# The operands of the first merge product requested during the last gate product

## The chip, the cores and the metric

The kernel runs on one core of a Trainium2 chip, as one program. The metric is the device time of one execution in microseconds (us), the median of several runs. Engines are named as in the profile: PE (TensorE's matmuls; its weight loads are listed as PEld), DVE (VectorE), ACT (ScalarE), POOL (GpSimd) and SP (SyncE, here the queue that issues most DMAs).

## What is computed

A decoder layer with three gated token mixers side by side, then cross-attention and an MLP. The change lies where the mixers are merged:

```python
u = rms_norm(h, norm_mix)
proj = u @ w_in
y_b = ssd_branch(...) @ w_ssd_out          # 2048 inner channels
y_c = swa_branch(...) @ w_attn_out         # sliding-window attention, 16 heads
gates = sigmoid(proj[..., OFF_GATE:] + gate_bias)     # 3 x 1024 columns
merged = gates[0] * y_a + gates[1] * y_b + gates[2] * y_c
h = h + merged @ w_mix_out
...
```

All is float32, 1024 tokens, model width 1024.

## The kernel before

Activations lie channel by channel: a [128, 1024] tile holds 128 channels of 1024 tokens, and a width of 1024 is eight such tiles. A float32 product is made of three products of rounded parts. An operand x is split into `oh`, a rounded copy written by ACT, and `ol`, the rest, written by DVE (`split`, lines 291 to 300: L295 and L296). A weight is split in the same way into `wh` and `wl` (`wslot`, L162 and L165 to L168). PE then adds wh x oh, wh x ol and wl x oh. `gemm_steps` does this for one output tile of 128 channels: for each of eight input tiles six matmuls of 512 tokens, and it yields after every third. So one product of 1024 x 128 has 16 steps, and two steps use up one input tile.

The normalised input u occupies eight pairs of split tiles: four in the pool `opa`, four in `opb`, and these pools have no other buffers. All products with u read them. Last among these are the 24 gate products. 21 of them (`gates_of`, 3 to 23) have no place of their own: they are filler. The generator `fillers` runs through them and then through `merge_head`, and the sliding-window attention calls `fill(n)` between its own small products, which advances the filler by 2n steps. A gate ends with a tanh on ACT (L324) into a tile `gate_th` of the pool `gp` (tag "glu", two buffers) and a store to `d_th` (L325).

`merge_head` is the beginning of the merge: the first two output tiles of y_b's first half. Its operands are the eight tiles `d_yb[0..7]`, which the SSD stage has stored to DRAM. For each one it requests a staging tile `yin` (even ones in `gp`, tag "glu", the gates' own; odd ones in `attn2`, two buffers), loads it (L336), and splits it into a pair of `opa` or `opb` (L295, L296). Those are the buffers that u holds until the last gate, number 23, has read them.

The attention goes through 16 blocks (8 groups of 128 queries, 2 halves of the heads). Iteration i transposes the probabilities of block i (`ps_pt`, L77, 8 at a time, twice; ACT copies them out, L1076), makes the scores of block i+2 (`ps_lg`, twice 8), and multiplies block i-1 by the values (`ps_o`). Between these stands one filler step each, four in an iteration. On the scores DVE adds the bias and takes the maximum (L1042) and makes the negated maximum `nm` and the sink's exponent `es` (L1050, L1051); ACT takes the exponentials (L1054, eight instructions); DVE sums and inverts (L1058, L1060); POOL multiplies the block `lg` by the inverse (L1061). All of these small products and the transposes share four PSUM buffers (`pss`). Gate 23 occupies iterations 10 to 13; `merge_head` begins in iteration 14, has eight of its 32 steps in iterations 14 and 15, and the rest at `fill(200)` after the attention.

What sets the order: PE's instructions are pinned in the order in which the program writes them (`Ordered`, `keep_in_program_order`). For the other engines a scheduler fixes the order beforehand. What is written in a `high_priority` block goes ahead of the rest as soon as its data and a buffer are there; a tile takes a buffer of its pool and tag when one is free. Each engine and each queue works through its list in order.

Of the kernel before, what the change touches and what calls it, by code (L numbers as in the profile page):

```python
# [9 lines left out]
F32 = mybir.dt.float32  # L10
# [7 lines left out]
P = 128  # L18
D = 1024
KT = D // P  # L20
T = 1024
# [7 lines left out]
START_GATES = 3  # L29
# [26 lines left out]
def trunk_kernel(tc, w_io):  # L56
    nc = tc.nc
    act, dve, pool = nc.scalar, nc.vector, nc.gpsimd
    ctx = ExitStack()
    with ctx:  # L60
# [57 lines left out]
        def C(name, i=0, n=1):  # L118
            o, w = _C[name]
            assert i + n <= w  # L120
            return cst[:, o + i:o + i + n]
# [9 lines left out]
        d_yb = dram.tile([16, P, T], F32, name="d_yb")  # L131
# [53 lines left out]
        def gemm_steps(slots, xh, xl, nk, pss_):  # L185


            for k in range(nk):
                wh, wl = slots(k)
                n = 0  # L190
                for stat, movs in ((wh, (xh, xl)), (wl, (xh,))):
                    for mv in movs:
                        for h in range(2):
                            sl = slice(h * 512, h * 512 + 512)
                            pe.matmul(
                                pss_[:, sl], stat, mv(k)[:, sl],
                                start=(k == 0 and stat is wh and mv is xh),
                                stop=(k == nk - 1 and stat is wl),
                            )
                            n += 1  # L200
                            if n % 3 == 0:
                                yield
# [8 lines left out]
        def ch_slots(src, cuts=(0, 1024)):  # L211
            wh, wl = wslot(src, cuts=cuts)
            return lambda k: (wh[:, k * P:(k + 1) * P], wl[:, k * P:(k + 1) * P])
# [71 lines left out]
        opa = ctx.enter_context(tc.tile_pool(name="opa", bufs=4))  # L285
        opb = ctx.enter_context(tc.tile_pool(name="opb", bufs=4))
        def pair(pool_):
            return (
                pool_.tile([P, T], F32R, tag="oh", name="oh"), pool_.tile([P, T], F32R, tag="ol", name="ol"),
            )  # L290

        def split(pool_, src, scale=None):
            a, b = pair(pool_)
            if scale is None:
                act.copy(a, src)  # L295
                dve.tensor_sub(b, src, a.bitcast(F32))  # L296
            else:
                act.activation(a, src, AF.Copy, scale=scale)
                dve.scalar_tensor_tensor(b, src, scale, a.bitcast(F32), ALU.mult, ALU.subtract)
            return a, b  # L300

        def hi(parts):
            return lambda k: parts[k][0]

        def lo(parts):
            return lambda k: parts[k][1]
# [4 lines left out]
        with ExitStack() as s1:  # L311
# [1 line left out]
            u = [pair(opa if k < 4 else opb) for k in range(KT)]  # L313
            UH, UL = hi(u), lo(u)

            def gates_of(n):
                for gt in n:
                    ps = pg.tile([P, T], F32, tag="g", name="ps_g")
                    steps = gemm_steps(ch_slots(w_io["w_ch"][40 + gt]), UH, UL, KT, ps)
                    for k in range(2 * KT):  # L320
                        next(steps)
                        if k == 2 * KT - 1:
                            th = gp.tile([P, T], F32, tag="glu", name="gate_th")
                            act.activation(th, ps, AF.Tanh, bias=C("gate_b", gt), scale=0.5)  # L324
                            nc.sync.dma_start(d_th[gt], th)  # L325
                        yield

            merging, staging = [], [gp]

            def merge_head():  # L330

                parts = []
                for k in range(KT):
                    with tc.high_priority():
                        y = staging[k % 2].tile([P, T], F32, tag="glu", name="yin")
                        nc.sync.dma_start(y, d_yb[k])  # L336
                        parts.append(split(opa if k < 4 else opb, y))
                two = [pg.tile([P, T], F32, tag="g", name="ps_g") for i in range(2)]
                sts = [gemm_steps(ch_slots(w_io["w_b0"][i]), hi(parts), lo(parts), KT, two[i]) for i in range(2)]
                merging.append((parts, two))  # L340
                for k in range(KT):
                    for st in sts:
                        for i in range(2):
                            next(st)
                            yield

            def fillers():
                yield from gates_of(range(START_GATES, 24))
                yield from merge_head()

            gates = fillers()

            filled = [0]
# [42 lines left out]
            with ExitStack() as sc:  # L396
# [117 lines left out]
                for s in range(4):  # L514

                    ps = pg.tile([P, T], F32, tag="g", name="ps_kv").rearrange("p (a b) -> p a b", b=512)
                    for kp in range(4):
# [5 lines left out]
                        for kk in range(2):  # L523
                            k = kp * 2 + kk
# [595 lines left out]
        with ExitStack() as sc:  # L1120
# [81 lines left out]
            parts = [split(opa if ct < 4 else opb, yconv[:, ct, :]) for ct in range(8)]  # L1202
# [5 lines left out]
        with tc.tile_pool(name="mix", bufs=2) as tp:  # L1208
            parts = [split(opa if i < 4 else opb, ht[i], 0.5) for i in range(KT)]
# [506 lines left out]
def build(nc, packed):  # L1716
    io = {k: nc.dram_tensor(k, v.shape, mybir.dt.from_np(v.dtype), kind="ExternalInput").ap() for k, v in packed.items()}
    io["outT"] = nc.dram_tensor("outT", (KT, P, T), F32, kind="ExternalOutput").ap()
    with tile.TileContext(nc) as tc:
        trunk_kernel(tc, io)  # L1720
# [12 lines left out]
```

## Time and profile before

| | us |
|---|---|
| runs before, median of 3 | 2727.51 |
| lowest, highest | 2725.08, 2733.04 |
| the profiled execution, time | 2729.99 |
| its span in the trace | 2728.0 |

The profiled execution took 2729.99 us, of which the trace shows a span of 2728.0 us. Times in the rows are microseconds from the start of the span. A row of the timeline reads: start, duration, engine, line, operation, tile written <- tiles read, shapes, count; in brackets how long the engine stood idle before it and what ended that. A row of the waits reads: who waited for whom, total, number, longest. A row of the stretches gives, for each engine in the order PE, PEld, DVE, ACT, POOL, its busy time and the number of its instructions, then the granted clock of TensorE as a share of the full one, the DMA engines' busy share and GB/s.

### The profile page before, as it was taken

Reading aid. Unit: us, or ns where it says so; the run is one execution under the profiler, and the core shown is the slowest. Engines: PE = TensorE matmul, PEld = TensorE weight load, DVE = VectorE, ACT = ScalarE, POOL = GpSimd, SP = SyncE. Lnnn points to the kernel's source line nnn. Section 1 sums busy time; section 2 is a strip of 40 time slices with the busy share of each in tenths; the row PEclk is TensorE's granted clock in tenths of the full one; section 3 lists DMA queues with packets and bytes.
Section 4 is the critical chain, followed back from the end, with each engine's and each line's share of the span. In section 5 each row is a group of like instructions: output and inputs, shape, how many; then the busy total and the mean of one; then the engine's idle time right before and its main releaser. Section 6 shows DMA issues by size and latency. Waiting matters only on the chain. (4 is left out here: it accounts for less than half of the span.)

```text
span 2728.0 us, 32485 instructions
## 1 busy us (share of the span) xinstructions
PE 2692.6 (99%) x12720; PEld 2180.4 (80%) x12720; DVE 1574.1 (58%) x1875; ACT 1097.1 (40%) x1827; POOL 794.1 (29%) x442
## 2 busy tenths in 40 slices
PE   9999999999999999999999999999998999999999
PEld 7888878888787878775588778899777888888887
DVE  7588878758667776524414774323368876532423
ACT  6533321225666666557611351235433332222221
POOL 2322221200504050424342422321115664422220
PEclk9999999999999999999999999999999999999999
DMA  7642232333555555572444332211123332454531
GB/s 241 210 128 97 97 112 88 123 124 85 147 162 143 145 151 153 177 218 82 149 170 160 101 109 100 101 55 40 47 77 116 139 131 106 175 194 142 202 137 70
DMA packets 119576, 354.83 MB, mean 130 GB/s; under 512 B 12016, under 2 KB 37120, under 8 KB 119040
## 3 DMA queue, kind: packets, MB, share of 16 engines
q1 hardware_dynamic: 112656, 328.12, 34.6%
q0 software_dynamic: 6768, 24.64, 5.2%
q8 instruction: 100, 1.64, 0.2%
q14 instruction: 52, 0.43, 0.1%
HBM read 277.06 MB, written 78.80 MB: 130 GB/s over the span
## 5 line engine op out<-in xcount | busy, mean ns | idle before, releaser
L73 PE MATMUL ps_g<-oh,wh 128*128 128x512 f32 x1776 | 575.8, 404 | 8.5 <-ACT oh L295 3.9
L73 PE MATMUL ps_g<-ol,wh 128*128 128x512 f32 x1776 | 562.0, 394 | 3.5 <-DVE ol L296 2.4
L73 PE MATMUL ps_g<-oh,wl 128*128 128x512 f32 x1776 | 552.0, 391 | 1.2 <-POOL wl L168 1.2
L168 POOL TENSOR_TENSOR wl<-ws,wh 128x1024 fp32r<-128x1024 f32 (+2 forms) x106 | 261.9, 2473 | 725.4 <-ACT wh L162 678.2
L73 PEld LDWEIGHTS ps_g<-ol,wh 128*128 128x128 f32 x1776 | 333.8, 188 | 85.5 <-issue 9.3
L73 PEld LDWEIGHTS ps_g<-oh,wl 128*128 128x128 f32 x1776 | 334.1, 188 | 72.8 <-POOL wl L168 1.6
L73 PEld LDWEIGHTS ps_g<-oh,wh 128*128 128x128 f32 x1776 | 321.4, 189 | 72.9 <-issue 10.3
L390 DVE SCALAR_TENSOR_TENSOR tapy<-hin,cst,tapy 128x1024 f32<-128x1024 f32 x240 | 354.6, 1478 | 31.7 <-ACT tapy L385 25.2
L162 ACT CAST wh<-ws 128x1024 fp32r<-128x1024 f32 (+1 forms) x169 | 176.4, 1044 | 464.8 <-PE ps_g L73 296.2
L73 PE MATMUL ps_up<-blk,st 128*128 128x512 f32 x1344 | 310.4, 393 | 8.6 <-DVE blk L1384 5.7
L73 PEld LDWEIGHTS ps_up<-blk,st 128*128 128x128 f32 x1344 | 254.7, 190 | 63.6 <-DVE blk L1384 6.3
L73 PE MATMUL ps_tm<-wh,oh 128*128 128x512 f32 (+1 forms) x704 | 253.9, 361 | 1.9 <-DVE ht L1225 0.6
L73 PE MATMUL ps_tm<-wh,ol 128*128 128x512 f32 (+1 forms) x704 | 246.8, 351 | 0.0
L73 PE MATMUL ps_tm<-wl,oh 128*128 128x512 f32 (+1 forms) x704 | 246.6, 350 | 0.0
L296 DVE TENSOR_TENSOR ol<-r_in,oh 128x1024 fp32r<-128x1024 f32 x64 | 94.0, 1473 | 220.6 <-ACT oh L295 220.6
L73 PE MATMUL ps_d<-ol,wh 128*128 128x512 f32 x512 | 199.4, 390 | 0.4 <-DVE ol L296 0.2
L73 PE MATMUL ps_d<-oh,wl 128*128 128x512 f32 x512 | 199.2, 389 | 0.0
L73 PE MATMUL ps_d<-oh,wh 128*128 128x512 f32 x512 | 199.2, 389 | 0.0
L73 PEld LDWEIGHTS ps_tm<-wh,oh 128*128 128x128 f32 x704 | 132.9, 189 | 21.8 <-issue 1.4
L166 POOL DMA_DIRECT2D wl<-w_ch x45 | 39.2, 870 | 378.3 <-ACT wl L165 378.2
L73 PEld LDWEIGHTS ps_tm<-wl,oh 128*128 128x128 f32 x704 | 133.0, 189 | 18.9 <-issue 1.4
L73 PEld LDWEIGHTS ps_tm<-wh,ol 128*128 128x128 f32 x704 | 132.9, 189 | 17.7
(372 smaller groups left out, 3767.4 us busy)
## 6 DMA issues: line engine op xcount, KB each, us to landing
r_in<-d_r SPq DMA_DIRECT2D x64, 512.0 KB, 4.1
ws<-w_ch SPq DMA_DIRECT2D x63, 512.0 KB, 3.5
wl<-w_ch POOLq DMA_DIRECT2D x45, 512.0 KB, 5.7
csb<-d_cs SPq DMA_DIRECT2D x32, 512.0 KB, 4.0
gth<-d_th SPq DMA_DIRECT2D x32, 512.0 KB, 4.3
ws<-w_up SPq DMA_DIRECT2D x32, 512.0 KB, 3.2
d_r<-r SPq DMA_DIRECT2D x32, 512.0 KB, 2.6
ws<-w_down SPq DMA_DIRECT2D x32, 512.0 KB, 3.3
```

The lines of the kernel that those rows point to most:

```text
L73: ins = nc.tensor.matmul(*a, **k)
L162: act.copy(wh[:, a:b], st[:, a:b])
L166: pool.dma_start(wl[:, a:b], src[:, a:b], accum_op=ALU.add)
L168: (low or pool).tensor_sub(wl[:, a:b], st[:, a:b], wh[:, a:b].bitcast(F32))
L296: dve.tensor_sub(b, src, a.bitcast(F32))
L390: dve.scalar_tensor_tensor(y, hin[:, j:j + T], w(j), y, ALU.mult, ALU.add)
```

## The change

The eight requests, loads and splits leave `merge_head` and become a function `merge_part(k)`. `gates_of` gets a callback: in the last gate of its range, after the second step of input tile k, it calls `passed(k)`. So request k is written right behind the matmuls that read u[k] for the last time. The tanh tile of gate 23 is requested after parts 0 to 6 and before part 7; before, it was requested ahead of all eight. The number of instructions, of DMAs and of buffers is the same, and so is PE's order.

```diff
-            def gates_of(n):
+            def gates_of(n, passed=lambda k: None):
+
                 for gt in n:
...
                             nc.sync.dma_start(d_th[gt], th)
+                        if k % 2 and gt == n[-1]:
+                            passed(k // 2)
                         yield
 
             merging, staging = [], [gp]
 
+            merge_parts = []
+
+            def merge_part(k):
+                with tc.high_priority():
+                    y = staging[k % 2].tile([P, T], F32, tag="glu", name="yin")
+                    nc.sync.dma_start(y, d_yb[k])
+                    merge_parts.append(split(opa if k < 4 else opb, y))
+
             def merge_head():
 
-                parts = []
-                for k in range(KT):
-                    with tc.high_priority():
-                        y = staging[k % 2].tile([P, T], F32, tag="glu", name="yin")
-                        nc.sync.dma_start(y, d_yb[k])
-                        parts.append(split(opa if k < 4 else opb, y))
+                parts = merge_parts
...
-                yield from gates_of(range(START_GATES, 24))
+                yield from gates_of(range(START_GATES, 24), merge_part)
```

## Rows read from the trace of the kernel before

**Rows 1.** The profile page, part 1: busy time of the engines in us, its share of the span and their instructions.

```profile
PE 2692.6 (99%) x12720; PEld 2180.4 (80%) x12720; DVE 1574.1 (58%) x1875; ACT 1097.1 (40%) x1827; POOL 794.1 (29%) x442
```

**Rows 2.** The waits of PE from 1295 to 1365 us, the longest.

```profile
PE ps_g L73 <- ACT oh L295: 3.9, 1, 3.9
```

**Rows 3.** Stretches: one iteration of the attention, then the wait and what follows it up to `fill(200)`.

```profile
1314.00:1323.40 9.40, 9.37 (x54) 5.45 (x52) 4.13 (x22) 6.17 (x21) 3.61 (x1) 1.00 0.09 29
...
1334.91:1338.85 3.94, 0.01 (x2) 0.00 (x1) 0.82 (x3) 3.65 (x13) 0.17 (x1) 0.95 0.64 188
1338.85:1345.04 6.19, 6.15 (x18) 4.65 (x19) 2.71 (x4) 4.98 (x12) 3.16 (x1) 0.50 0.87 310
1345.04:1356.04 11.00, 11.00 (x57) 5.83 (x55) 8.15 (x8) 7.36 (x10) 0.44 (x1) 0.99 0.60 198
```

**Rows 4.** The timeline of SP: the DMAs that it issues around the first and the last `yin` loads (the count is at the end of a row).

```profile
1192.01 0.80 SPq L336 DMA_DIRECT2D yin<-d_yb  x2
...
1295.52 0.32 SPq L325 DMA_DIRECT2D d_th<-gate_th  x1
1296.50 29.14 SPq L1093 DMA_DIRECT2D d_yc<-oT  x4
1325.73 0.46 SPq L336 DMA_DIRECT2D yin<-d_yb  x1
...
1340.08 8.17 SPq L336 DMA_DIRECT2D yin<-d_yb  x5
```

**Rows 5.** The timeline of ACT: the end of gate 23, the sink exponent that opens each block's exponentials, and the copies of the transposes.

```profile
1285.90 0.19 ACT L1052 ACTIVATE es<-es 128x8 f32<-128x8 f32 x1
...
1296.34 0.19 ACT L1052 ACTIVATE es<-es 128x8 f32<-128x8 f32 x1
...
1305.31 0.19 ACT L1052 ACTIVATE es<-es 128x8 f32<-128x8 f32 x1
...
1318.24 1.04 ACT L1076 COPY pT<-ps_pt 128x512 f32<-128x512 f32 x2
...
1332.55 1.11 ACT L324 ACTIVATE gate_th<-ps_g,cst 128x1024 f32<-128x1024 f32 x1
```

**Rows 6.** The tile `yin`: its splits, all 24 of the kernel in one row (shortest, median and longest in ns), and the landing of its loads.

```profile
L295 ACT CAST oh<-yin x24: 1029/1051/1060, 1337.8 to 1533.8; 128x1024 fp32r<-128x1024 f32 x24
L296 DVE TENSOR_TENSOR ol<-yin,oh x24: 1209/1224/2299, 1338.8 to 1534.8; 128x1024 fp32r<-128x1024 f32 x24
...
DMA to landing us min/median/max: 3.4/4.8/7.7
```

**Rows 7.** The timeline of PE in iteration 12 and on to `fill(200)`.

```profile
1318.85 1.14 PE L77 MATMUL ps_pt<-mat,lg 128*128 128x128 f32 x8
...
1333.82 1.09 PE L77 MATMUL ps_pt<-mat,lg 128*128 128x128 f32 x8
1338.85 1.22 PE L73 MATMUL ps_g<-oh,wh 128*128 128x512 f32 x2 [3.93 <-ACT oh L295]
...
1345.91 1.94 PE L73 MATMUL ps_o<-pT,vt 128*64 128x512 f32 x8
1347.78 1.09 PE L77 MATMUL ps_pt<-mat,lg 128*128 128x128 f32 x8
...
1356.04 0.74 PE L73 MATMUL ps_g<-oh,wh 128*128 128x512 f32 x2
...
1357.54 0.63 PE L73 MATMUL ps_g<-oh,wh 128*128 128x512 f32 x2
```

**Rows 8.** The timeline of DVE: the second half of the scores in iterations 11 and 12, then, of the last block, the sink's exponent and the sum.

```profile
1312.41 0.42 DVE L1042 CUSTOM_DVE_ANT_0 lg<-ps_lg,bias 128x256 f32<-128x256 f32 x1 [2.16 <-PE ps_lg L73]
...
1321.78 0.42 DVE L1042 CUSTOM_DVE_ANT_0 lg<-ps_lg,bias 128x256 f32<-128x256 f32 x1 [2.10 <-PE ps_lg L73]
...
1332.86 2.24 DVE L1051 TENSOR_TENSOR es<-nm,nsink 128x8 f32<-128x8 f32 x1
...
1341.26 0.17 DVE L1058 TENSOR_TENSOR rs<-rs,es 128x8 f32<-128x8 f32 x1
```

**Rows 9.** The timeline of POOL from iteration 11 on.

```profile
1309.78 3.61 POOL L1061 TENSOR_TENSOR lg<-lg,rd 128x2048 f32<-128x2048 f32 x1 [5.09 <-DVE rd L1060]
1319.21 3.61 POOL L1061 TENSOR_TENSOR lg<-lg,rd 128x2048 f32<-128x2048 f32 x1 [5.82 <-DVE rd L1060]
1328.58 3.61 POOL L1061 TENSOR_TENSOR lg<-lg,rd 128x2048 f32<-128x2048 f32 x1 [5.76 <-DVE rd L1060]
1332.72 2.36 POOL L168 TENSOR_TENSOR wl<-ws,wh 128x1024 fp32r<-128x1024 f32 x1 [0.54 <-ACT wh L162]
1341.88 3.60 POOL L1061 TENSOR_TENSOR lg<-lg,rd 128x2048 f32<-128x2048 f32 x1 [6.80 <-DVE rd L1060]
```

**Rows 10.** The line of `es` on DVE, all 16 of the kernel (shortest, median and longest in ns).

```profile
L1051 DVE TENSOR_TENSOR es<-nm,nsink x16: 166/168/2241, 1194.0 to 1332.9; 128x8 f32<-128x8 f32 x16
```

**Rows 11.** Stretches: two other waits of PE, the first from 1216.3 and the second from 2033.1 us, each with the stretch behind it.

```profile
1216.30:1218.70 2.40, 0.18 (x3) 0.09 (x2) 2.37 (x3) 1.65 (x2) 2.40 (x2) 1.00 0.89 263
1218.70:1222.10 3.40, 3.40 (x15) 2.57 (x17) 0.68 (x2) 3.29 (x14) 0.68 (x1) 0.54 1.01 282
...
2033.10:2035.70 2.60, 0.01 (x1) 0.01 (x1) 2.56 (x5) 0.00 (x0) 0.00 (x0) 1.00 0.00 0
2035.70:2040.00 4.30, 4.27 (x19) 3.58 (x20) 4.26 (x6) 2.19 (x4) 0.00 (x0) 1.00 0.30 122
```

## The prediction

> **What bounds the kernel now.** I read the page first: PE is busy for 99% of the span [rows 1], so only what makes PE wait, or slows its clock, can move the time. The waits of PE then name one place where the change can act: near 1339 us PE waits 3.9 us for the rounded copy `oh` of a merge operand [rows 2]. The stretches show what it costs. PE stands still from 1334.91 to 1338.85, and behind that the granted clock is 0.50, the lower of its two levels (1.2 instead of 2.4 GHz), for 6.19 us [rows 3]. Work of 6.2 us at half clock is worth 3.1, so stall and clock together cost 3.9 + 3.1 = 7.0 us, or 0.26% of the time. That is the ceiling of the direct gain. About 0.3%, or 8.2 us, is what a measurement of this kernel can tell from no change.
>
> Why was the operand late? SP's rows tell it. Two loads of `yin` went out at 1192.0, and the next only at 1325.7, although the store of gate 22, whose buffer it takes, was issued at 1295.5 [rows 4]. The early two must be the odd ones, with `attn2` for themselves. Tile 0 shares `gp` with the gates, and gate 23's tanh, written ahead of it, ran at 1332.6 [rows 5]. I read this as buffers of one tag being handed out in the order of the requests: tile 0 could be asked for only when tanh 23 had been given its place in the schedule, and the split of tile 1 stood behind that of tile 0. By this reading the change acts. Request 0 now stands behind gate 22 and loads soon after 1295; tiles 2, 4 and 6 follow as `gp` buffers come free, and each split follows once gate 23 is past its u[k].
>
> **What the change moves.** Eight loads on SP, eight casts on ACT of 1.05 us and eight subtractions on DVE of 1.22 us [rows 6] go from iterations 14 and 15 to iterations 10 to 13, two of each per iteration. Nothing is added or removed. SP: a load takes 3.4 to 7.7 us to land [rows 6], and two steps of the gate pass about every 4.7 us, half of the 9.4 us iteration [rows 3], so loads stay ahead. In SP's queue they stand among the `d_yc` stores, four of which are all that SP issues from 1296.5 to 1325.7 [rows 4]; a load that waits for its buffer can hold up only a store, and no engine waits for the stores there. I cost it at nothing; if it failed, one load's 4.8 us would be seen as a wait of ACT.
>
> *The end, from 1334.9 on.* PE comes out of the transposes of block 14 at 1334.91 with operand 0 ready. Six merge matmuls take 1.5 us, counted from rows at full clock, transposes 1.1, six more 1.5, the values 1.9 [rows 7]: PE would reach the transposes of block 15 at 1340.9. They need block 15 scaled by POOL. That chain is: `es` ends at 1335.1, held up by POOL's weight subtraction (L168) [rows 8, 9]; eight exponentials of 0.5 us without the two casts that now stand between them, so 1339.3; then 0.6 from the sum to POOL's start (1341.26 to 1341.88), and 3.6 on POOL [rows 8, 9]. So 1343.6, a new wait of 2.7 us. From these transposes to the end of the attention's products takes 8.3 us (1347.78 to 1356.04) [rows 7], so the end falls at 1351.9, and the gain shrinks from 7.0 to 4.2 us before anything is paid for.
>
> *Operand 0 (iteration 10).* Its cast falls among the exponentials and puts them off by about 1 us. The nearest row is the end of gate 22, where three ACT operations put them off: the openings of the exponentials stand 10.4 and then 9.0 us apart (1285.90, 1296.34, 1305.31) instead of 9.4 twice [rows 5], so 0.6 us are lost. I take 0.6; the bounds are 0 and 1.05, the whole cast.
>
> *Operands 2, 4 and 6 (iterations 11 to 13).* u[4] is free when step two of iteration 12 ends, at 1318.8 [rows 7]. ACT copies transposes from 1318.24 on [rows 5], so the cast ends between 1319.9 and 1320.4 and the subtraction is DVE's next instruction. But POOL scales a block from 1319.21 to 1322.82 [rows 9]. What that does to DVE shows at `es`, a subtraction of two tiny SBUF operands: normally 0.17 us, once 2.24 [rows 10], and that one began at 1332.86 and ended with POOL's operation at 1335.1 [rows 8, 9]. So do the splits of `yin`, 1.22 us as a rule and up to 2.30 [rows 6]. L1042, which reads scores from PSUM, isn't touched: it takes 0.42 beside POOL's work [rows 8]. So the subtraction ends at 1322.82 + 1.22 = 1324.04, and the second half of the scores, which began at 1321.78 [rows 8], stands behind it: 2.26 us late. In iteration 11 the same sum is 1309.78 + 3.61 + 1.22 - 1312.41 = 2.20 [rows 8, 9]. Behind these scores the exponentials are late by as much, then the copies of the transposes, then PE: it starts the second transposes of an iteration at 1318.85, only 0.6 us after the copies begin [rows 5, 7], so there is no slack. Two iterations at 2.2 are 4.4 us; the bounds are 0 (the subtraction gets through before POOL or after the scores) and 2.6 each, as POOL has 3.6 + 1.2 us less some 2.2 of DVE's idle time [rows 8]. In iteration 13 the same delay puts the scores back to 1333.4, but there L168 held `es` until 1335.1 anyway; it now starts behind the subtraction, at 1333.4 instead of 1332.7 [rows 9]. That costs 0.7 at block 15, whose wait becomes 3.4 us.
>
> *Operands 1, 3, 5 and 7.* Their u[k] comes free half an iteration later, near 1323, when POOL has finished (1322.82) [rows 9] and ACT, busy for 6.2 of 9.4 us in an iteration [rows 3], waits for the scores: I take nothing; the upper bound is the 0.2 by which a cast could reach into the exponentials.
>
> *The clock.* A wait of 3.4 us at block 15 lies between a wait of 2.2 us which was followed by 3.4 us at half clock (0.54) and the 3.9 with 6.2 us of it; one of 2.6 us at 2033 was followed by none [rows 3, 11]. I take 1.7 us, half of 3.4; the bounds are 0 and 3.1.
>
> Sum: -4.2 + 0.6 + 4.4 + 0.7 + 1.7 = +3.2 us. On the profiled execution's own 2729.99 that gives 2733.2. That execution lies 2.5 us above the median of 2727.51, so against the median I predict 2730.7, a change of 0.12%, which counts as no change.
>
> **The rivals.**
> - *The splits get through, faster but within 0.3%.* If the scheduler puts the subtractions behind the scores, or if they reach DVE before POOL starts, the 4.4 and 0.7 fall away: -4.2 + 0.6 and 0 to 1.7 for the clock, so -3.6 to -1.9, near 2724.8. For it: DVE is idle for 2.1 us before the second scores [rows 8]. Against it: POOL's 3.6 us cover just that. Here a rule stands by itself: the Trainium skill, "SBUF — State Buffer", section "Who interferes with whom", says that issue order decides which of DVE and POOL is blocked for a whole instruction. By that rule POOL would be the one to wait if the subtraction came first, with the time of this rival; no row here shows that order.
> - *All of it is gained.* The exponentials of block 15 come early enough that no new wait appears: -7.0, 2720.5.
> - *Nothing moves.* Should buffers not be served in the order of requests, the splits stay where they are: 2727.5. The load at 1192 shows that priority does carry a request far ahead [rows 4]; that tile 0 wasn't carried speaks against it.
> - *Slower by more.* Each of the 2.2 us waits in iterations 11 and 12 is followed by 3.4 us at half clock, as the one at 1216 was [rows 11], and that at block 15 by 6.2: -4.2 + 0.6 + 4.4 + 0.7 + 2 x 1.7 + 3.1 = +8.0, so 2735.5 and, with the upper bounds of the other terms, beyond 2736. It decides if a wait of 2.2 us suffices each time.
>
> **How the numbers follow.** Forecast 0.43; splits get through 0.27; all gained 0.07; nothing moves 0.10; slower by more 0.13. The forecast's own range, by its bounds, is 2728 to 2734. With both neighbours it is 2721 to 2736.5; left out are the outer halves of "all gained" and of "slower by more" and some of each end for what a new order does elsewhere. Faster by over 0.3% (under 2719.3) only by more than the ceiling: 0.05. Slower by over 0.3% (above 2735.7): 0.12. Within: 0.83.
>
> **What would show it.** Right: the wait for L295 gone; casts between 1299 and 1334; the subtractions of operands 2 and 4 lasting 3 us or more beside L1061, `nm` some 2.2 us later behind them, PE waiting for L1076 after them and for L1061 at block 15. Wrong: subtractions of 1.2 us throughout, or scores ahead of them on DVE; no wait at block 15; casts still at 1337.

## The result, and the profile after

| | before | after |
|---|---|---|
| median of 19 runs, us | 2727.99 | 2733.74 |
| lowest, highest | 2725.08, 2733.04 | 2729.95, 2738.41 |
| span of the profiled execution | 2728.0 | 2732.4 |

The ratio after to before is 1.0021 with a 95% interval of 1.0015 to 1.0027: slower by 4 to 7 us, inside the forecast's 0.3%. The forecast was +3.2 us; the medians lie 5.75 us apart, and 2733.74 is just inside the upper end of the forecast's own range, 2728 to 2734.

PE issues the same instructions in the same order in both kernels, so the traces can be laid on each other instruction by instruction, and the lag of each (its start after, less its start before) says where time was lost. An iteration is measured from its first transposes to the next iteration's; the last stretch runs from those of iteration 14 to the first product of `fill(200)`, which is at 1356.04 us in the kernel before [rows 7] and at 1359.34 after:

| stretch | 10 | 11 | 12 | 13 | 14 and 15 | sum |
|---|---|---|---|---|---|---|
| longer by, us | +1.03 | +0.70 | +2.15 | +2.15 | -0.84 | +5.19 |

The rest of the kernel, which the change doesn't touch, gives back 0.8 us: PE reaches iteration 10 1.9 us earlier than before, and behind `fill(200)` it loses 1.1, where a stretch of half clock near 2040 us falls, to which the last section comes back. The sum of the table is what has to be explained.

The change and the runs below move the lines behind them by a few: ACT's copies of the transposes are L1076 before, L1082 in the change and L1079 to L1085 in the runs, POOL's scaling is L1061, then L1067 to L1070. `oT` is DVE's copy of the attention's products out of PSUM.

The page's busy times are those of [rows 1] but for 3 us of PE and 8 of DVE, so something that DVE does takes longer:

```profile
PE 2695.7 (99%) x12720; PEld 2180.9 (80%) x12720; DVE 1582.3 (58%) x1875; ACT 1096.2 (40%) x1827; POOL 795.1 (29%) x442
```

The waits of PE from 1290 to 1365 us. The 3.9 us for L295 [rows 2] are gone; these stand there in their place, the longest for the tanh of the last gate:

```profile
PE ps_g L73 <- ACT gate_th L325: 2.8, 1, 2.8
PE ps_pt L77 <- ACT pT L1082: 2.8, 3, 0.9
PE ps_lg L73 <- DVE oT L1098: 1.1, 2, 0.5
PE ps_pt L77 <- DVE oT L1098: 0.7, 1, 0.7
PE ps_lg L73 <- ACT pT L1082: 0.4, 1, 0.4
```

SP's timeline of the `yin` loads. The two at 1190 are the odd ones again. The even ones, which went out from 1325.7 on [rows 4], now go out from 1291.6 on. So the change acts as it was meant to:

```profile
1190.16 0.80 SPq L338 DMA_DIRECT2D yin<-d_yb  x2
...
1291.56 0.38 SPq L338 DMA_DIRECT2D yin<-d_yb  x1
...
1300.07 6.01 SPq L338 DMA_DIRECT2D yin<-d_yb  x3
...
1314.32 3.23 SPq L338 DMA_DIRECT2D yin<-d_yb  x2
```

The tile `yin` (shortest, median, longest in ns, then first and last start). The casts are as long as before; the longest subtraction went from 2.30 us [rows 6] to 3.58, which the subtractions of operands 2, 4 and 6 take:

```profile
L295 ACT CAST oh<-yin x24: 1034/1051/1057, 1298.0 to 1536.4; 128x1024 fp32r<-128x1024 f32 x24
L296 DVE TENSOR_TENSOR ol<-yin,oh x24: 1209/1224/3583, 1299.1 to 1537.5; 128x1024 fp32r<-128x1024 f32 x24
```

POOL's and DVE's timelines say when that happens. POOL:

```profile
1300.78 3.59 POOL L1067 TENSOR_TENSOR lg<-lg,rd 128x2048 f32<-128x2048 f32 x1 [5.06 <-DVE rd L1066]
1309.60 3.60 POOL L1067 TENSOR_TENSOR lg<-lg,rd 128x2048 f32<-128x2048 f32 x1 [5.23 <-DVE rd L1066]
...
1336.85 2.73 POOL L168 TENSOR_TENSOR wl<-ws,wh 128x1024 fp32r<-128x1024 f32 x1 [0.59 <-ACT wh L162]
1344.70 3.60 POOL L1067 TENSOR_TENSOR lg<-lg,rd 128x2048 f32<-128x2048 f32 x1 [5.12 <-DVE rd L1066]
```

DVE: the subtraction of operand 0 and `nm` in iteration 10, then the subtraction of operand 2 in iteration 11 and what stands behind it:

```profile
1299.06 1.23 DVE L296 TENSOR_TENSOR ol<-yin,oh 128x1024 fp32r<-128x1024 f32 x1 [0.82 <-ACT oh L295]
...
1302.78 1.62 DVE L1056 SCALAR_TENSOR_TENSOR nm<-mx,nsink 128x8 f32<-128x8 f32 x1
...
1310.71 3.58 DVE L296 TENSOR_TENSOR ol<-yin,oh 128x1024 fp32r<-128x1024 f32 x1 [0.63 <-ACT oh L295]
1314.21 0.41 DVE L1048 CUSTOM_DVE_ANT_0 lg<-ps_lg,bias 128x256 f32<-128x256 f32 x1
...
1315.90 0.17 DVE L1057 TENSOR_TENSOR es<-nm,nsink 128x8 f32<-128x8 f32 x1
```

The subtraction of operand 2 begins 1.11 us after POOL's scaling and ends at 1314.29, 1.09 after the scaling's end (1309.60 + 3.60 = 1313.20): as if it stood still beside POOL and did nearly all its work behind it. DVE's work on the second scores begins only then (1314.21). In iterations 12 and 13 the subtractions of operands 4 and 6 show the same picture. The stretch of one iteration, to be held against the first of [rows 3], and PE's timeline:

```profile
1314.82:1326.35 11.53, 10.05 (x54) 5.73 (x52) 8.72 (x24) 8.05 (x23) 3.60 (x1) 1.00 0.38 114
```

```profile
1314.91 1.09 PE L77 MATMUL ps_pt<-mat,lg 128*128 128x128 f32 x8
...
1320.83 1.14 PE L77 MATMUL ps_pt<-mat,lg 128*128 128x128 f32 x8 [0.95 <-ACT pT L1082]
...
1326.43 1.09 PE L77 MATMUL ps_pt<-mat,lg 128*128 128x128 f32 x8
...
1345.10 1.22 PE L73 MATMUL ps_g<-oh,wh 128*128 128x512 f32 x2 [2.84 <-ACT gate_th L325]
...
1351.08 1.09 PE L77 MATMUL ps_pt<-mat,lg 128*128 128x128 f32 x8
...
1359.34 0.74 PE L73 MATMUL ps_g<-oh,wh 128*128 128x512 f32 x2
```

The wait for POOL's scaling of block 15 that was forecast for the end isn't there: the transposes at 1351.08 start without a wait. PE stands still earlier, from 1342.26 on, for the PSUM buffer of gate 23, which the second output tile of the merge takes over. ACT's timeline says why its tanh was late, and the stretches what followed:

```profile
1335.73 1.05 ACT L162 CAST wh<-ws 128x1024 fp32r<-128x1024 f32 x1 [1.04 <-PE ps_g L73]
1336.68 1.04 ACT L295 CAST oh<-yin 128x1024 fp32r<-128x1024 f32 x1
1339.90 0.21 ACT L1058 ACTIVATE es<-es 128x8 f32<-128x8 f32 x1 [2.19 <-DVE es L1057]
...
1343.95 1.09 ACT L325 ACTIVATE gate_th<-ps_g,cst 128x1024 f32<-128x1024 f32 x1
```

```profile
1342.26:1345.10 2.84, 0.00 (x0) 0.00 (x1) 0.37 (x2) 2.84 (x10) 0.40 (x1) 0.75 0.90 264
1345.10:1350.52 5.42, 5.42 (x12) 2.59 (x14) 0.00 (x0) 1.85 (x4) 3.20 (x1) 0.50 0.61 206
```

Before, the tanh ran at 1332.55, ahead of block 15's `es` [rows 5, 8]. Now the cast of operand 7 and the eight exponentials of block 15 stand ahead of it in ACT's list, and ACT idles 2.19 us for `es`, part of which is due to DVE's third blocked subtraction (run 2 has 1.62 without it), with the tanh standing behind. PE stands still for 2.84 us, and the granted clock is 0.50, the lower level, for the 5.42 behind it.

### The profile page after: what moved, and what is told of

It is laid out like the page before. It is cut to its first block, busy times and chain, and to the rows that moved or that the text cites. A ratio compares the mean times of both kernels' runs of the same rounds, so it can differ in the third digit from the quotient of the medians.

```text
span 2732.4 us, 32490 instructions
## 1 busy us (share of the span) xinstructions
PE 2695.7 (99%) x12720; PEld 2180.9 (80%) x12720; DVE 1582.3 (58%) x1875; ACT 1096.2 (40%) x1827; POOL 795.1 (29%) x442
## 5 line engine op out<-in xcount | busy, mean ns | idle before, releaser
L296 DVE TENSOR_TENSOR ol<-r_in,oh 128x1024 fp32r<-128x1024 f32 x64 | 94.3, 1477 | 220.4 <-ACT oh L295 220.4
```

## The experiments

Two questions. Is it DVE's subtraction beside POOL that lengthens iterations 12 and 13 (the theory), or are it the casts, which put off ACT's work (the rival)? And is the lost gain at the end the tanh's place, or would any order pay there? The kernels below leave PE's order as it is. Each row of this table gives the ratio to the kernel before with its interval, and the stretches as above:

| run | ratio | 10 | 11 | 12 | 13 | 14, 15 | sum |
|---|---|---|---|---|---|---|---|
| the change | 1.0021 (1.0015 to 1.0027) | +1.03 | +0.70 | +2.15 | +2.15 | -0.84 | +5.19 |
| 1 subtractions behind `es` | 0.9996 (0.9987 to 1.0005) | +0.97 | +0.13 | +0.20 | +0.19 | -2.42 | -0.93 |
| 2 no scaling on POOL | one run | +0.94 | -0.32 | +0.19 | +0.19 | -2.37 | -1.37 |
| 3 tanh first | 1.0012 (1.0002 to 1.0022) | +1.03 | +0.69 | +2.16 | +2.15 | -3.61 | +2.42 |
| 4 two early | 0.9999 (0.9989 to 1.0008) | +1.03 | +0.69 | +0.01 | 0.00 | -4.13 | -2.40 |
| 5 = 1 and 3 | 0.9994 (0.9985 to 1.0003) | +0.94 | +0.16 | +0.17 | +0.19 | -4.17 | -2.71 |
| 6 = 5, casts behind copies | 0.9984 (0.9975 to 0.9993) | -0.01 | +0.15 | +0.19 | +0.18 | -4.18 | -3.67 |
| 7 two early, behind both | 0.9987 (0.9978 to 0.9996) | +0.02 | +0.14 | 0.00 | 0.00 | -4.13 | -3.97 |
| 8 = 6, last scaling on DVE | 0.9986 (0.9977 to 0.9995) | 0.00 | +0.15 | +0.18 | +0.18 | -5.54 | -5.03 |

The stretches come from one profiled execution of each kernel and agree between kernels to some hundredths where these do the same; the whole time scatters by several us, so the ratios tell apart only the larger steps. The first four expectations number an iteration by its subtraction, the table by where PE loses the time, which is one later: what they call iterations 11 and 12 are the columns 12 and 13.

### 1. The subtractions behind the sinks' exponent

The requests come in pairs, the last pair ahead of the tanh's, and DVE's list has each subtraction behind the subtraction `es` of its iteration instead of ahead of the second scores. The lists of ACT, SP, POOL and PE are those of the change.

```diff
-                    dve.tensor_sub(es, nm, nsink[:, sk])
+                    sinks.append(dve.tensor_sub(es, nm, nsink[:, sk]))
...
-                    merge_parts.append(split(opa if k < 4 else opb, y))
+                    with tc.issue_after(sinks[-1].ins):
+                        merge_parts.append(split(opa if k < 4 else opb, y))
```

> The changed kernel, with one thing moved: on DVE each iteration's two subtractions of merge operands stand behind that iteration's es instead of where they became ready; the lists of ACT, SP, POOL and PE are those of the changed kernel. Theory A (DVE's subtraction is blocked while POOL scales a block, and the scores stand behind it): all subtractions take 1.2 us, iterations 11 and 12 shrink from 11.5 to 9.4 to 10.0 us, and the time falls by 3.5 to 4.5 us against the changed kernel, to about 2729.5. Theory B (the two casts of 1.05 us an iteration on ACT, ahead of the copies and the exponentials, make the 2.15 us): ACT's list is the same, so the iterations stay at 11.5 and the time within 1 us of 2733.7. Theory C (the late tanh of gate 23 and the half clock behind it are the cost): as B.

Measured: 2727.32 us, ratio 0.9996 (0.9987 to 1.0005). That is 6.4 us less than the change, where 3.5 to 4.5 were expected: beside iterations 12 and 13 (3.9 us by the table), iteration 11 gets 0.6 and the end 1.6 us shorter. All eight subtractions take 1.22 us (the line L296 in this stretch), and iterations 12 and 13 lose 0.2 us each instead of 2.15:

```profile
L296 DVE TENSOR_TENSOR ol<-yin,oh x8: 1210/1218/1219, 1303.6 to 1335.5; 128x1024 fp32r<-128x1024 f32 x8
```

The casts stand where they stood, so it isn't they that make the 2.15. At the end PE still waits for the tanh, 1.7 us, with 3.4 us near half clock behind it (the waits, then the stretch from the wait's end):

```profile
PE ps_g L73 <- ACT gate_th L327: 1.7, 1, 1.7
PE ps_pt L77 <- DVE oT L1099: 1.3, 1, 1.3
```

```profile
1339.60:1343.00 3.40, 3.31 (x8) 2.12 (x10) 0.00 (x0) 1.95 (x5) 3.30 (x1) 0.51 0.71 283
```

### 2. The change without POOL's scaling

The multiplication of `lg` by the inverse sums is left out in all blocks, so the probabilities aren't normalised. The other engines' lists are those of the change.

```diff
-                    pool.tensor_mul(
-                        lg[:, :, k0:], lg[:, :, k0:], rd.unsqueeze(2).to_broadcast([P, 8, kn])
-                    )
```

> The changed kernel without POOL's multiplication of the attention's blocks by the inverse of their sums, so the probabilities go on unscaled; the lists of ACT, DVE, SP and PE are the same as in the changed kernel, with the subtractions ahead of the second half of the scores. Theory A: nothing reads SBUF on POOL in iterations 10 to 12, so the subtractions of operands 2 and 4 take 1.2 instead of 3.6 us and iterations 11 and 12 shrink from 11.5 to 9.4 to 9.9 us. Theory B: 11.5 as before, since the casts stand where they stood. Theory C tells nothing of the iterations and expects the wait for tanh 23 of 2.8 us unchanged.

Measured: 2722.39 us in one run. The subtractions stand on DVE where the change put them, ahead of the second scores, and take 1.23 us at most:

```profile
L296 DVE TENSOR_TENSOR ol<-yin,oh x8: 1212/1226/1226, 1295.2 to 1330.2; 128x1024 fp32r<-128x1024 f32 x8
```

Iterations 12 and 13 lose 0.19 us each. With experiment 1 this settles the first question from both sides: with either of the two taken away, the subtraction's place or POOL's scaling, 0.2 us an iteration are left of the 2.15. The 0.70 of iteration 11 go in both runs too (+0.13 and -0.32). Iteration 10 still loses 0.94, and the wait for the tanh is still 2.84 us; neither is POOL's doing.

### 3. The tanh of gate 23 first

Only the tanh of the last gate and its store are written with priority, so that ACT runs it ahead of cast 7 and of block 15's exponentials.

```diff
-                            th = gp.tile([P, T], F32, tag="glu", name="gate_th")
-                            act.activation(th, ps, AF.Tanh, bias=C("gate_b", gt), scale=0.5)
-                            nc.sync.dma_start(d_th[gt], th)
+                            with tc.high_priority() if gt == n[-1] else ExitStack():
+                                th = gp.tile([P, T], F32, tag="glu", name="gate_th")
+                                act.activation(th, ps, AF.Tanh, bias=C("gate_b", gt), scale=0.5)
+                                nc.sync.dma_start(d_th[gt], th)
```

> The changed kernel with the tanh of gate 23 (tile, activation, store) in a high-priority block, which puts it ahead of the sink exponent and the eight exponentials of block 15 on ACT and changes little else. Theory A holds two costs apart: the iterations 11 and 12 stay at 11.5 us, the wait of 2.8 us for tanh 23 goes, and PE instead waits 2 to 3 us for POOL's scaling of block 15 before its transposes; end of the attention 1 to 3 us earlier than in the changed kernel, time about 2731.5 (2730.5 to 2733). Theory C: the whole loss goes, 2728 or less.

Measured: 2731.29 us, ratio 1.0012 (1.0002 to 1.0022). Iterations 10 to 13 cost what they cost in the change, to 0.01 us. The last stretch gives -3.61 instead of -0.84, and the longest single waits of PE are others:

```profile
PE ps_pt L77 <- POOL lg L1068: 1.8, 1, 1.8
PE ps_o L73 <- ACT pT L1083: 1.8, 1, 1.8
```

So the tanh's place cost 2.8 us. On DVE a copy `oT` moved along, ahead of the subtraction of operand 7, and the wait of 0.7 us for it is gone as well; how much is due to which wasn't tried apart. What is late next are the copies of block 14's transposes and POOL's scaling of block 15, the wait that had been forecast.

### 4. Only operands 0 and 1 early

Operands 2 to 7 are requested in `merge_head` without priority.

```diff
-            def merge_part(k):
-                with tc.high_priority():
+            def merge_part(k, how=None):
+                with how or tc.high_priority():
...
+                for k in range(2, KT):
+                    merge_part(k, ExitStack())
                 parts = merge_parts
...
-                yield from gates_of(range(START_GATES, 24), merge_part)
+                yield from gates_of(range(START_GATES, 24), lambda k: merge_part(k) if k < 2 else None)
```

> Operands 0 and 1 requested during the last gate as in the changed kernel; operands 2 to 7 requested in the merge's head as before, but without high priority, so that they stand behind the exponentials of block 15. Theory A: iterations 11 and 12 at 9.4 us, 1.0 to 1.8 us lost at operands 0 and 1, no wait for L295 at the merge's first product, a wait of 2.5 to 3 us for POOL's scaling of block 15 with or without half clock behind it; end of the attention 0.5 to 3 us earlier than in the kernel before, time 2725 to 2728. Theory B: the same sign, since two casts remain of eight. Theory C: the tanh runs ahead of the exponentials as before, the whole of the first wait is gained, 2721.

Measured: 2727.41 us, ratio 0.9999 (0.9989 to 1.0008). Operands 0 and 1 cost 1.72 us in iterations 10 and 11 as in the change, iterations 12 and 13 cost nothing, and the last stretch gives all of -4.13: the tanh, with no early cast 7 ahead of it, keeps its place. Six of the eight early operands brought nothing that PE could use.

### 5 and 6. Both remedies together, and the casts behind the copies

Run 5 joins the edits of 1 and 3. Run 6 adds that each cast stands behind the copies of the transposes of its iteration on ACT:

```diff
-                    with tc.issue_after(sinks[-1].ins):
+                    with tc.issue_after(sinks[-1].ins), tc.issue_after(turns[-1].ins):
                         merge_parts.append(split(opa if k < 4 else opb, y))
...
-                            act.copy(pTs[b, j], pt)
+                            turns.append(act.copy(pTs[b, j], pt))
```

> The requests come in pairs, each DVE subtraction stands behind the subtraction of its iteration's sinks (as in the run with that alone), and the tanh of gate 23 comes first on ACT at the end of attention (as in the run with that alone). Theory (two separate costs, which add): iterations 10 to 13 keep what the first of the two runs had against the kernel before, +0.97, +0.13, +0.20, +0.19 us, and iterations 14 and 15 what the second had, -3.61; no PE wait for the tanh, no half clock there, two waits of about 1.8 us left; sum -2.1 us, about 2725.9. Rival (what is taken away at one place is found again at the next): iterations 14 and 15 give no more than the -2.42 of the first run or fall back to half clock, sum -0.9 or above, 2727 or more. Fallen for both if iterations 12 and 13 lengthen by over 0.5 us again.

> As the run with both, and besides ACT's casts stand behind the four pT copies of their iteration, so that none falls among the exponentials or between the copies. Theory (operand 0 and 1 cost PE 1.1 to 1.7 us because a cast of 1.05 us delays the last exponential and the copies that PE waits for): iterations 10 and 11 together fall from +1.1 to 0.4 us or less, the waits of PE for pT copies go, and iterations 12 and 13 stay at +0.2 each or less; sum -2.8 to -3.2 us, about 2725. Rival (it is the DVE's subtractions or the loads that cost iteration 10, not the cast): iteration 10 stays at +0.9 to +1.0 and the time is that of the run with both.

Measured, run 5: 2727.19 us, ratio 0.9994 (0.9985 to 1.0003). The stretches bear out the theory: iterations 10 to 13 as in run 1, and at the end even a little more than in run 3, -4.17. The ratio alone couldn't tell it from run 1, and the median is what the rival had named, 2727 or more.

Run 6: 2724.37 us, ratio 0.9984 (0.9975 to 0.9993), faster than before. Iteration 10 falls from +0.94 to -0.01. ACT's timeline in that iteration: the last exponential, the four copies, then cast 0 and cast 1:

```profile
1298.97 0.49 ACT L1062 ACTIVATE lg<-lg,nm 128x256 f32<-128x256 f32 x1
1299.46 2.00 ACT L1084 COPY pT<-ps_pt 128x512 f32<-128x512 f32 x4
1301.36 1.06 ACT L295 CAST oh<-yin 128x1024 fp32r<-128x1024 f32 x1
1302.61 1.05 ACT L295 CAST oh<-yin 128x1024 fp32r<-128x1024 f32 x1 [0.20 <-PE ps_g L73]
```

That this moved iteration 10 and nothing else says that the cast ahead of the last exponential was the cost there. The waits of PE that are left from 1290 to 1362 us:

```profile
PE ps_pt L77 <- POOL lg L1069: 1.9, 1, 1.9
PE ps_o L73 <- ACT pT L1084: 0.9, 1, 0.9
PE ps_pt L77 <- DVE oT L1100: 0.2, 1, 0.2
```

### 7. Two early, behind both

The edit of run 4 with the two casts behind the copies and the two subtractions behind `es`, requested together after u[1].

```diff
-                yield from gates_of(range(START_GATES, 24), lambda k: merge_part(k) if k < 2 else None)
+                yield from gates_of(range(START_GATES, 24), lambda k: [merge_part(j) for j in (0, 1)] if k == 1 else None)
```

> Only operands 0 and 1 are asked for early, their casts behind the pT copies and their subtractions behind the subtraction of that iteration's sinks; operands 2 to 7 are asked for after the gate, in the order of their own. Theory: no cost in iterations 10 to 13 (0.3 us in all or less), and the -4.1 us of iterations 14 and 15 that the run with two early requests had; sum about -3.8 us, 2724.2. Rival (the end of attention needs more of the operands early to gain): iterations 14 and 15 give less than 3 us once nothing is late before them, sum about -2.5, no better than that run, which was 0.9999 of the kernel before.

Measured: 2724.47 us, ratio 0.9987 (0.9978 to 0.9996). Iterations 10 to 13 cost 0.16 us in all, and the end gives -4.13. Two operands early are as good as eight.

### 8. The last scaling on DVE

Run 6 with the scaling of block 15, and of that block alone, on DVE.

```diff
-                    pool.tensor_mul(
+                    (dve if (n, half) == order[-1] else pool).tensor_mul(
                         lg[:, :, k0:], lg[:, :, k0:], rd.unsqueeze(2).to_broadcast([P, 8, kn])
                     )
```

> As the run with the casts behind the copies, but the last scaling of the attention (block 15, 128x2048) runs on DVE instead of POOL; nothing else moves. Theory (what is left at the end of attention is POOL's scaling of block 15, 3.6 us, for which PE waits 1.9 us): on DVE it takes about twice the 1.22 us of a 128x1024 subtraction, 2.4 us, so that wait falls by about 1.2 to 0.7 us and iterations 14 and 15 give -5.4 instead of -4.2; sum -4.9, about 2723. Rival (another wait is as late: the pT copies of block 14, or ACT's exponentials of block 15 in front of the scaling): the wait moves to another line, iterations 14 and 15 stay at -4.2 to -4.5 and the time is that of the run with the casts behind the copies.

Measured: 2724.39 us, ratio 0.9986 (0.9977 to 0.9995). The scaling takes 2.29 us instead of 3.60, the wait for it 0.5 instead of 1.9, and the last stretch gives -5.54 (the line of the scaling on DVE, then the waits of PE):

```profile
L1069 DVE TENSOR_TENSOR lg<-lg,rd x1: 2291/2291/2291, 1340.1 to 1340.1; 128x2048 f32<-128x2048 f32 x1
```

```profile
PE ps_o L73 <- ACT pT L1084: 0.9, 1, 0.9
PE ps_pt L77 <- DVE lg L1069: 0.5, 1, 0.5
```

So POOL's scaling ate about half of what run 6 still missed of the ceiling of 7.0 us at the end, 1.4 of 2.8. The 1.4 us that the trace shows are not to be seen in the median, which equals that of run 6 within its scatter.

## Why the prediction was right, and where it wasn't

That the change makes the kernel slower by less than 0.3%, and the main term, were right; the sum was 2.0 us short of what the traces show (+3.2 against +5.19), by two steps. The forecast's end of block 15's scaling, 1343.6, adds up to 1343.5 from its own rows, which changes nothing.

- **The change acts** by the order of requests, as read from [rows 4, 5]: the even loads go out from 1291.6 us. "Nothing moves" fell.
- **Operands 2 and 4: right, in mechanism and size.** Forecast 2.20 and 2.26 us, measured 2.15 in each of two iterations, and by experiments 1 and 2 shown to be DVE beside POOL. The Trainium skill, "SBUF — State Buffer", section "Who interferes with whom", has DVE and POOL lock each other out of the ports they share, by order of issue. The trace agrees, both ways round: the subtraction of operand 6 ran to 1337.34 us, and POOL's weight subtraction, begun beside it at 1336.85, took 2.73 us where the median of its five is 2.39; `nm`, begun beside that at 1338.75, took 0.85 us, to within 0.02 of its end (POOL's line, then DVE's timeline). The rival in which the subtraction gets there first needs an order that the scheduler didn't choose; run 1, which gives the subtraction a place behind the scores, is the other half of that rival.

```profile
L168 POOL TENSOR_TENSOR wl<-ws,wh x5: 2389/2395/2729, 1336.9 to 1398.8; 128x1024 fp32r<-128x1024 f32 x5
1333.76 3.58 DVE L296 TENSOR_TENSOR ol<-yin,oh 128x1024 fp32r<-128x1024 f32 x1 [0.63 <-ACT oh L295]
...
1338.75 0.85 DVE L1056 SCALAR_TENSOR_TENSOR nm<-mx,nsink 128x8 f32<-128x8 f32 x1
```

- **Operand 0: mis-sized, 1.73 us instead of 0.6.** The forecast took the row at the end of gate 22 as the nearest; its bound, the whole cast, was the truth: iteration 10 lost 1.03 us, and run 6 shows that it is the cast. The other 0.70, in iteration 11, had no term: operand 1 was costed "nothing, at most 0.2". In the trace of after the sum of block 11 stands behind the subtraction of operand 0 (1299.06 + 1.23), so POOL's scaling starts late against the scores, and `nm`, whose operands lie in SBUF, takes 1.62 us beside it, where it took 0.58 before (the row below). Putting the subtractions behind `es` (run 1) or both behind the copies and `es` (run 7) leaves 0.13 and 0.14, and without POOL's scaling (run 2) nothing is lost. So it is the same contention at a place where I hadn't looked for it; that it goes through `nm` is read from the timelines and wasn't tried by itself.

```profile
1304.13 0.58 DVE L1050 SCALAR_TENSOR_TENSOR nm<-mx,nsink 128x8 f32<-128x8 f32 x1
```

- **The end of the attention: the step "a new wait of 2.7 us" for block 15 named the wrong wait.** The chain that I followed, exponentials, sum, POOL, was the chain that is late next, but only in a kernel whose tanh stays where it was. "Nothing is added or removed" hid that eight casts with priority move what has none: cast 7 and the exponentials went ahead of gate 23's tanh on ACT, and the merge's second output tile needs that gate's PSUM buffer. The stretch gave -0.84 us, where -4.2 + 0.7 + 1.7 = -1.8 were forecast. Once the tanh has its place back the forecast's own terms are met: -4.17, -4.18 and -4.13 in runs 5 to 7 against -4.2, and -3.61 in run 3, which still has iteration 13's delay, against -4.2 + 0.7 = -3.5. But the 2.7 us come there in two waits, in run 6 0.9 for the copies of block 14 and 1.9 for POOL. In run 8 the wait for the scaling is down to 0.5 and the stretch gives -5.54 of the ceiling of 7.0.
- **The clock: near its upper bound, and in place by luck.** I took 1.7 us; 5.42 us of work at the lower level cost 2.7. It came behind the tanh's wait, not behind block 15's: the waits of 1.8 and 1.9 us that stand there in runs 3 to 7 were followed by none. So a term for the clock belonged in the sum for a reason that the forecast didn't have.

The books close: against the forecast, operands 0 and 1 cost 1.1 more, operands 2 and 4 together 0.1 less, the end gave 1.0 less; that is 2.0. "All gained" fell with the waits, and "slower by more" because no half clock followed the delays in iterations 12 and 13, where PE's waits are 0.95 us at most.

## What to carry to other kernels

Work that is brought forward with priority is costed on every engine by what it now stands ahead of: not only what waits for it, but each ordinary instruction that it pushes back, and who holds a buffer until that one has run. Here a DVE operation with two operands in SBUF has to be placed by POOL's timetable: the same subtraction cost 0.2 us at most behind `es` and 2.15 in front of the scores. And here, where the merge uses two operands before the attention ends, two early were as good as eight; the other six only brought their costs forward.

## What the hardware showed that I had not expected

A wait's length alone didn't tell here whether half clock follows. The wait of 2.84 us for the tanh was followed by 5.42 us at 0.50, that of 1.70 us in run 1, behind one of 1.3, by 3.4 at 0.51; in run 3 two waits of 1.8 us, one soon after the other, leave the whole stretch at 1.00:

```profile
1336.00:1355.00 19.00, 15.33 (x85) 9.22 (x81) 5.67 (x16) 9.36 (x27) 5.62 (x2) 1.00 0.44 138
```

And the wait of 2.60 us near 2033 us, followed by none before [rows 11], was followed in the kernel after, where it is 2.63 us long and nothing near it was changed, by a stretch at 0.58 that begins 1.0 us behind its end (the matmuls that end the wait, then the stretch):

```profile
2038.52 0.70 PE L73 MATMUL ps_g<-oh,wh 128*128 128x512 f32 x2 [2.63 <-DVE ht L1350]
...
2039.50:2042.90 3.40, 3.40 (x10) 2.65 (x9) 3.37 (x6) 2.18 (x4) 0.00 (x0) 0.58 0.29 118
```

Why one is and the other isn't stays open; no run here was made for it.
